# The unused tile ahead of the weight pool of a hybrid block's last stages: 96 bytes in place of 480

## The chip, the cores and the metric

The kernel runs on one core of a Trainium2 chip. The metric is the time of one execution on the device in microseconds; lower is better. Before the change three runs took 2,879.13 to 2,882.53 us, with a median of 2,881.99 us.

## What is computed

One layer of a diffusion backbone over 1,024 latent tokens and 256 context tokens with 1,024 channels. Per layer: a feed-forward part with half weight, a token mixer (grouped attention beside a gated linear recurrence, HGRN2, in both directions), and a second feed-forward part. Cut to what matters here:

```python
def swiglu(u, w_gate, w_up, w_down):
    return (jax.nn.silu(u @ w_gate) * (u @ w_up)) @ w_down
def merge(p, o_att, o_hg, w_att_out_l, w_hg_out_l, w_o_l):
    y = jax.nn.sigmoid(p[8]) * (o_att @ w_att_out_l) + jax.nn.sigmoid(p[9]) * (o_hg @ w_hg_out_l)
    return y @ w_o_l
...
x = x + ffn1(x, mx)
...
y_x, y_c = token_mixer(...)
x = x + post(y_x, norm_post[l, 1], mx[5])
...
x = x + ffn2(x, mx)
```

The hidden width of the feed-forward parts is 2,816, that is 22 slices of 128. The context tokens take part in the first feed-forward part and in the mixer; the merge and the second feed-forward part are computed for the latent tokens alone.

## The kernel before, in words

Activations lie transposed, channels on the 128 partitions and tokens along the free dimension, in chunks of 512, 512 and 256 (context) tokens. Every large product is made three times: operands are split into a high and a low part in the type float32r, and `term` (lines 98 to 102) issues high x high (line 100), high weight x low activation (line 101) and low weight x high activation (line 102). Each is one 128x128 stationary tile, loaded anew for each matmul, and a moving tile of 512 columns (256 for the context and for the last pieces). `load_w` (lines 86 to 93) fetches a weight of 128x1,024 floats with one DMA into the staging tile `st`, ScalarE casts the high part (line 91) and VectorE subtracts to get the low part (line 92); both are tiles `w` of 4,096 bytes a partition of the pool that is named by the caller.

The stages, in order: the first FFN (weights from the pool `w1`); the attention, with projections as fillers between its matmuls (`fb`, weights from `w1`); the HGRN stage, with the gate columns as fillers (`fb`, weights from the pool `hgw`); and the last stages, in which all weights come from the pool `ffn2w`: the merge (line 1046 on, moving tiles `h00` to `l11`, called `h` and `l` in the rows), the output projection `w_o` and the second FFN (moving tiles `uh`, `ul`, and `h` for the down projection). The merge begins when the last `fb` fillers are done. During the output projection the norms of the chunks that are done run beside it on VectorE, ScalarE and GpSimd (`Norms.chain`, lines 244 to 286; `cb`, `rc` and `acc` are their tiles), moved forward piece by piece by `nrm.pump()`; the second FFN of a chunk starts when its norm has written `uh` and `ul`. A Tile framework places the tiles, sets the waits and orders each engine's instructions; each engine works through its own queue.

**Where tiles lie.** Pools are stacks in each partition's memory: those without a side grow from the low addresses, those with `side="right"` from the top at byte 229,344 down. Lines 1039 to 1043 open the right stack of the last stages:

```python
    w2_ctx = ExitStack()
    edge = w2_ctx.enter_context(tc.tile_pool(name="edge", bufs=1, side="right"))
    edge.tile([P, 120], F32, name="edge")
    wp = w2_ctx.enter_context(tc.tile_pool(name="ffn2w", bufs=12, side="right", reuse_waits="tile"))
```

Nothing reads or writes the tile `edge`; it takes 480 bytes, from 228,864 to the top. Below it lie the twelve slots of `ffn2w`, from 179,712 to 228,864, each at a multiple of 512 bytes. The slots of `w1` lie from 83,328 to 124,288 and those of `hgw` from 83,328 to 99,712, each at a multiple of 512 plus 384. So do the moving tiles: `uh0` at 5,504, `uh1` at 21,888, `ul0` at 38,272, `ul1` at 54,656, the merge's `h` and `l` tiles from 103,808 on, the first FFN's `h` tiles from 136,576 on and the second's from 138,624 on: all leave 384 modulo 512. A stationary slice steps by 512 bytes within its slot, a moving slice by 2,048 bytes within its tile. The exceptions are the context's `uh2` and `ul2` (480 modulo 512, 256 columns). The highest tile of the left stack in the merge (`gt`) ends at 179,584. Before `ffn2w`, the memory of its slots belonged to tiles of the HGRN stage (`qt`, `q2`, `k1`, `qb`, `Sp`, `kt`, `s0`, `both`, `ss`, `sq`, `rr`); a new tile waits until the tiles that it covers are no longer read.

## Time and profile before

| what | value |
|---|---|
| median of three runs | 2,881.99 us |
| the profiled execution | 2,881.1 us |
| its span, first to last instruction | 2,879.3 us |
| mean granted TensorE clock | 0.982 |
| TensorE matmuls busy | 2,750.9 us, 96% |
| VectorE, ScalarE, GpSimd busy | 54%, 35%, 12% |

The profile is one execution. PE stands for TensorE's matmuls, PEld for its weight loads, DVE for VectorE, ACT for ScalarE, POOL for GpSimd, SP for the engine that issues DMAs. In rows of groups, `out<-in` are the program's tiles and x is the count. Matmuls are pipelined: the next one starts before the last one's row ends, so the distance between starts, not the length of a row, tells how fast they are taken.

### The profile page before, as it was taken

What the parts mean: (1) busy time and instruction counts of PE and PEld (TensorE: products, weight loads), DVE (VectorE), ACT (ScalarE), POOL (GpSimd) and SP (SyncE); (2) the same over time, 40 slices, a digit from 0 to 9 for tenths busy, and PEclk for the clock granted to TensorE, in tenths of its full rate; (3) what the DMA queues carried; (4) which work ended last, traced back from release to release, by engine and by line L of the source; (5) the groups of instructions that cost most, each with busy time, mean ns of one, the idle gap of its engine ahead of it and who ended that gap; (6) DMA issues with size and microseconds to landing.
All of it is one profiled execution on the core that took longest, in us unless ns stands there. A gap on an engine that the chain in (4) does not pass through costs nothing.

```text
span 2879.3 us, 37319 instructions
## 1 busy us (share of the span) xinstructions
PE 2750.9 (96%) x15032; PEld 2336.6 (81%) x15032; DVE 1543.3 (54%) x2893; ACT 1010.0 (35%) x1495; POOL 354.7 (12%) x276
## 2 busy tenths in 40 slices
PE   4799999999999989999999988899999999999998
PEld 3588888888888888889988877788778888888887
DVE  7756554444435885655654398645464333333336
ACT  3521111111112542667775565244354211111123
POOL 4700000000000332100000232212131000000002
PEclk9899999999999999999999999999999999999999
DMA  6553222332212332111111333164343211111123
GB/s 228 178 155 96 74 81 73 95 96 74 66 44 88 116 109 77 61 59 40 38 55 55 115 115 120 63 197 142 122 147 104 67 49 44 45 44 56 47 68 102
DMA packets 114702, 259.48 MB, mean 90 GB/s; under 512 B 12256, under 2 KB 51808, under 8 KB 114528
## 3 DMA queue, kind: packets, MB, share of 16 engines
q1 hardware_dynamic: 114528, 257.08, 28.3%
q8 instruction: 118, 1.93, 0.3%
q14 instruction: 56, 0.46, 0.0%
HBM read 216.67 MB, written 40.37 MB: 89 GB/s over the span
## 4 chain that ended last, share of the span: by engine, by line
PE 75%; DVE 9%; issue 8%; ACT 4%; POOL 2%; DMA 2%; SPq 0%; DVEq 0%; POOLq 0%; ACTq 0%
PE bank L101 13%; PE bank L102 13%; PE bank L100 13%; PE y L100 6%; PE y L101 6%; PE y L102 6%; PE fb L102 3%; PE fb L101 3%; PE fb L100 3%; PE S L749 2%; PE bank L765 1%; PE po L778 1%; PE po L779 1%; DVE acc L242 1%; DVE w L92 1%
## 5 line engine op out<-in xcount | busy, mean ns | idle before, releaser
L100 PE MATMUL bank<-uh,w 128*128 128x512 f32 (+1 forms) x1952 | 718.7, 369 | 17.2 <-ACT uh L460 14.7
L101 PE MATMUL bank<-ul,w 128*128 128x512 f32 (+1 forms) x1952 | 721.9, 370 | 6.8 <-POOL ul L461 6.8
L102 PE MATMUL bank<-uh,w 128*128 128x512 f32 (+1 forms) x1952 | 720.8, 369 | 2.1 <-DVE w L92 2.1
L91 ACT CAST w<-st 128x1024 fp32r<-128x1024 f32 x234 | 242.9, 1047 | 798.2 <-PE y L101 442.6
L100 PEld LDWEIGHTS bank<-uh,w 128*128 128x128 f32 x1952 | 370.7, 190 | 81.8 <-ACT uh L460 17.0
L101 PEld LDWEIGHTS bank<-ul,w 128*128 128x128 f32 x1952 | 372.0, 191 | 72.6 <-POOL ul L461 9.9
L102 PEld LDWEIGHTS bank<-uh,w 128*128 128x128 f32 x1952 | 372.5, 191 | 64.6 <-DVE w L92 2.7
L92 DVE TENSOR_TENSOR w<-st,w 128x1024 fp32r<-128x1024 f32 x212 | 267.9, 1271 | 260.2 <-ACT w L91 258.2
L355 DVE TENSOR_TENSOR y<-y,y 128x512 f32<-128x512 f32 (+1 forms) x416 | 255.1, 619 | 206.4 <-PE y L102 204.4
L100 PE MATMUL y<-h,w 128*128 128x512 f32 (+1 forms) x736 | 284.3, 389 | 8.0 <-ACT h L341 3.6
L101 PE MATMUL y<-h,w 128*128 128x512 f32 (+1 forms) x736 | 282.8, 384 | 0.3 <-DVE h L342 0.3
L102 PE MATMUL y<-h,w 128*128 128x512 f32 (+1 forms) x736 | 281.9, 384 | 0.6 <-DVE w L92 0.6
L340 DVE TENSOR_TENSOR sl<-bank,sl 128x512 f32<-128x512 f32 (+1 forms) x114 | 70.5, 620 | 380.3 <-PE bank L102 372.7
L268 POOL TENSOR_TENSOR y<-y,xt 128x512 f32<-128x512 f32 x48 | 64.2, 1355 | 1570.4 <-DVE y L267 885.5
L100 PE MATMUL fb<-uh,w 128*128 128x512 f32 (+1 forms) x576 | 222.4, 386 | 0.0
L102 PE MATMUL fb<-uh,w 128*128 128x512 f32 (+1 forms) x576 | 219.7, 381 | 0.0
L101 PE MATMUL fb<-ul,w 128*128 128x512 f32 (+1 forms) x576 | 219.7, 381 | 0.0
L100 PEld LDWEIGHTS y<-h,w 128*128 128x128 f32 x736 | 138.0, 188 | 42.0 <-ACT h L341 5.1
L102 PEld LDWEIGHTS y<-h,w 128*128 128x128 f32 x736 | 138.5, 189 | 29.6 <-DVE w L92 1.3
L101 PEld LDWEIGHTS y<-h,w 128*128 128x128 f32 x736 | 138.8, 189 | 26.7 <-DVE h L342 0.6
L341 ACT CAST h<-sl 128x512 fp32r<-128x512 f32 (+1 forms) x92 | 55.4, 602 | 283.9 <-DVE sl L340 283.7
L339 ACT ACTIVATE sl<-bank 128x512 f32<-128x512 f32 (+1 forms) x114 | 61.3, 539 | 191.2 <-PE bank L102 191.1
(225 smaller groups left out, 4315.9 us busy)
## 6 DMA issues: line engine op xcount, KB each, us to landing
st<-in_w_mod SPq DMA_DIRECT2D x77, 512.0 KB, 3.7
st<-in_w_gate SPq DMA_DIRECT2D x56, 512.0 KB, 3.7
st<-in_w_up SPq DMA_DIRECT2D x56, 512.0 KB, 3.7
st<-in_w_down SPq DMA_DIRECT2D x56, 512.0 KB, 3.6
st<-in_w_col SPq DMA_DIRECT2D x32, 512.0 KB, 3.7
gate_d<-ft SPq DMA_DIRECT2D x32, 256.0 KB, 2.3
gt<-gate_d SPq DMA_DIRECT2D x32, 256.0 KB, 2.7
st<-in_w_o SPq DMA_DIRECT2D x16, 512.0 KB, 3.7
```

The source lines that it names most:

```text
L91: act.copy(hi, st)
L92: eng.tensor_tensor(lo, st, f32(hi), op=ALU.subtract)
L100: pe.matmul(ps, lh, rh, start=first, stop=False)
L101: pe.matmul(ps, lh, rl, start=False, stop=False)
L102: pe.matmul(ps, ll, rh, start=False, stop=last)
L242: dve.tensor_tensor(a3, a3, sq, op=ALU.add)
L268: pool.tensor_tensor(yj, yj, xt, op=ALU.add)
L339: act.activation(sl, pg, AF.Silu)
L340: dve.tensor_tensor(sl, pu, sl, op=ALU.mult)
L341: act.copy(hh, sl)
L355: dve.tensor_tensor(yd, py, yd, op=ALU.add)
L749: pe.matmul(S[:, cs_], qT[:, (s * 2 + t) * P:(s * 2 + t + 1) * P], kT[g][:, cs_], start=(s == 0), stop=(s == 1))
```

## The change

The unused tile has 24 floats in place of 120, 96 bytes in place of 480. All slots of `ffn2w` move up by 384 bytes, to addresses that leave 384 modulo 512.

```diff
-    edge.tile([P, 120], F32, name="edge")
+    edge.tile([P, 24], F32, name="edge")
```

## Rows read from the trace of the kernel before

**Rows 1.** The page, part 1: busy time and share of the span.

```profile
PE 2750.9 (96%) x15032; PEld 2336.6 (81%) x15032; DVE 1543.3 (54%) x2893; ACT 1010.0 (35%) x1495; POOL 354.7 (12%) x276
```

**Rows 2.** By stretch: us; busy PE, PEld, DVE, ACT, POOL; granted clock, DMA share, GB/s.

```profile
1860.00:1985.00 125.00, 125.00 (x585) 103.61 (x584) 56.42 (x80) 50.09 (x71) 23.63 (x15) 1.00 0.52 167
...
2062.00:2177.00 115.00, 107.94 (x489) 88.15 (x487) 75.25 (x193) 67.16 (x112) 44.52 (x32) 0.94 0.44 138
2177.00:2790.00 613.00, 612.82 (x2637) 495.48 (x2636) 218.80 (x278) 109.01 (x142) 0.00 (x0) 1.00 0.18 55
```

**Rows 3.** Timeline of TensorE, first FFN: start us, length; the first and last of 83.

```profile
530.68 0.39 PE L100 MATMUL bank<-uh,w 128*128 128x512 f32 x1
...
549.27 0.39 PE L101 MATMUL bank<-ul,w 128*128 128x512 f32 x1
```

**Rows 4.** The same, last gate columns: the first and last of 54.

```profile
1905.00 0.39 PE L100 MATMUL fb<-uh,w 128*128 128x512 f32 x1
...
1917.02 0.40 PE L102 MATMUL fb<-uh,w 128*128 128x512 f32 x1
```

**Rows 5.** The same, merge: the first and last of 81.

```profile
1917.25 0.40 PE L100 MATMUL bank<-h,w 128*128 128x512 f32 x1
...
1935.85 0.39 PE L102 MATMUL bank<-h,w 128*128 128x512 f32 x1
```

**Rows 6.** The same, second FFN: the first and last of 174.

```profile
2299.79 0.39 PE L100 MATMUL y<-h,w 128*128 128x512 f32 x1
...
2340.00 0.39 PE L102 MATMUL bank<-uh,w 128*128 128x512 f32 x1
```

**Rows 7.** The same, first FFN, behind matmuls of 256 columns.

```profile
500.65 0.28 PE L102 MATMUL y<-hc,w 128*128 128x256 f32 x1
...
502.18 0.39 PE L102 MATMUL bank<-uh,w 128*128 128x512 f32 x1
...
502.64 0.40 PE L101 MATMUL bank<-ul,w 128*128 128x512 f32 x1
502.88 0.39 PE L102 MATMUL bank<-uh,w 128*128 128x512 f32 x1
...
503.57 0.39 PE L102 MATMUL bank<-uh,w 128*128 128x512 f32 x1
...
504.25 0.39 PE L102 MATMUL bank<-uh,w 128*128 128x512 f32 x1
...
505.61 0.39 PE L102 MATMUL bank<-uh,w 128*128 128x512 f32 x1
```

**Rows 8.** Groups of TensorE's matmuls by shape from 1,885 us on.

```profile
L100 PE MATMUL bank<-uh,w 128*128 128x512 f32 x800 | 317.7, 397 | 0.6 <-ACT sl L339 0.6
...
L100 PE MATMUL y<-h,w 128*128 128x512 f32 x336 | 133.0, 398 | 0.2 <-ACT h L341 0.2
...
L100 PE MATMUL bank<-h,w 128*128 128x512 f32 x128 | 50.5, 395 | 0.0
...
L102 PE MATMUL bank<-uh,w 128*128 128x256 f32 x64 | 18.0, 281 | 0.0
...
L101 PE MATMUL y<-h,w 128*128 128x256 f32 x32 | 9.1, 287 | 0.0
```

**Rows 9.** What TensorE waited for, 1,980 to 2,200 us.

```profile
PE cb L217 <- DVE rc L194: 3.8, 1, 3.8
PE bank L102 <- DVE w L92: 2.1, 1, 2.1
```

**Rows 10.** Timeline of TensorE behind the first of these waits.

```profile
2091.10 0.63 PE L102 MATMUL bank<-uh,w 128*128 128x512 f32 x1
...
2092.38 0.63 PE L102 MATMUL bank<-uh,w 128*128 128x512 f32 x1
```

**Rows 11.** Line 1021 on TensorE, and ScalarE's first cast of a merge weight.

```profile
L1021 PE MATMUL hb<-ident,sq x8: 270/272/273, 1883.7 to 1884.4; 128*128 128x128 f32 x8
...
1913.18 1.05 ACT L91 CAST w<-st 128x1024 fp32r<-128x1024 f32 x1 [1.18 <-DMA st<-in_w_mrg]
```

## The prediction

> **What bounds the kernel now.** I read the page's busy shares first, then the busy time by stretch, then the groups of the last stretch, and last the start times of single matmuls. TensorE is busy for 96% of the span [rows 1]. [...]

> A busy share of 100% doesn't say how fast the matmuls follow each other. They overlap (a row lasts 0.39 us, and the next one starts some 0.23 us after it), so what counts is the distance between two starts, the pitch. For matmuls of 512 columns I took it from four stretches that hold nothing else:
> - First FFN, from 530.68 to 549.27 us: 83 matmuls, 82 distances, 18.59 us, so 226.7 ns [rows 3].
> - Last gate columns (`fb`), from 1,905.00 to 1,917.02 us: 54 matmuls, 12.02 us over 53, so 226.8 ns [rows 4].
> - Merge, which begins right behind it, from 1,917.25 to 1,935.85 us: 81 matmuls, 18.60 us over 80, so 232.5 ns [rows 5].
> - Second FFN, from 2,299.79 to 2,340.00 us: 174 matmuls, 40.21 us over 173, so 232.4 ns [rows 6].

> The third and fourth lie on one side, the first and second on the other. Between the second and the third only a quarter of a microsecond passes. Both lie in one stretch at a granted clock of 1.00 [rows 2], and shape and type are the same; what changes is which tiles are read. The stationary tile comes from the pool `hgw` on the left in the second and from `ffn2w` on the right in the third. By the addresses given with the kernel, `hgw` and `w1` slots start at 384 modulo 512, like every moving tile of these four stretches, and `ffn2w` slots start at 0. All slices step by 512 or 2,048 bytes, so a slice has the remainder of its slot.

> A second trait goes with it. Where the remainders are equal, the pitch settles: behind a run of 256-column matmuls the starts 502.18 to 503.57 are 1.39 us for six distances, 231.7 ns each, and from 504.25 to 505.61 six distances take 1.36 us, 226.7 ns each [rows 7]. Where they are unequal, no such settling is left in a mean over 173.

> **The change, part by part.** The unused tile shrinks from 480 to 96 bytes. No instruction works on it, so nothing is added or removed on any engine or queue. The pool `ffn2w` is stacked below it and moves up by 384 bytes: its slots go from remainder 0 to 384, the remainder of the moving tiles `uh`, `ul`, `h` and of the merge's own `h` and `l` tiles. That is the whole change.

> *512-column matmuls of the last stages.* From 1,885 us on there are three lines each with 128 (merge), 800 (output projection, gate and up) and 336 (down) of them [rows 8]: 3 x 1,264 = 3,792. If they take the pitch of the equal stretches, each gains 232.45 - 226.75 = 5.7 ns. The sum is 3,792 x 5.7 ns = 21.6 us. The two ends for the pitch are 226.7 (settled) and 232.5 (nothing changes); I take the settled one, because the `fb` matmuls [rows 4] are nearest in time, with the same moving tiles `uh` and `ul` that the second FFN reads.

> *256-column matmuls.* There are 64 and 32 on each of three lines [rows 8], 288 in all. At the unequal remainders of now two of the groups have a mean length of 281 and 287 ns [rows 8]; a 256-column row at equal remainders lasts 0.28 us [rows 7]. No difference in length shows at this width, so I take 0, with 288 x 5.7 ns = 1.6 us more or less as an outer bound.

> *Settling.* After a break some ten matmuls run at about 231.7 instead of 226.7. The last stages have few breaks; eight of them would cost 8 x 10 x 5 ns = 0.4 us. I take 0.2.

> *The norm stretch, 2,062 to 2,177 us.* Here TensorE is busy for 107.94 of 115 us at a clock of 0.94 [rows 2]. It waits 3.8 us for VectorE's `rc` and 2.1 us for the split weights `w` [rows 9]. [...] The chain that it waits for runs on VectorE, ScalarE and GpSimd, which this change doesn't speed up. So what the matmuls of this stretch gain may turn into a longer wait. The stretch has 489 matmuls [rows 2], the norm's small ones among them; an estimate of 400 wide ones gives 400 x 5.7 ns = 2.3 us. Bounds: all kept, or all lost. I take half, 1.2 us lost, since there are full runs as well as waits in it. The chain begins only when the matmuls ahead are done, so what is gained before it is kept.

> *Memory that is taken over.* Shifted by 384 bytes, three weight slots lie over other remains of the HGRN stage: the second weight tile that the pool gives out now touches its `rr`, the third its `sq` and `ss`, the fourth its `both`. The last work that reads any of these is TensorE's transposes of `sq`, which start from 1,883.7 to 1,884.4 us [rows 11]. The first cast of a merge weight is at 1,913.18 us [rows 11], so 28 us cover that, and I cost it at nothing. Without that cover it would be a wait of ScalarE's cast behind the transposes, and the merge weights would be late.

> *Sum.* 21.6 - 0.2 - 1.2 = 20.2 us. The profiled execution took 2,881.1 us, 1.8 us more than its span of 2,879.3 us; 0.9 us less than the median of 2,881.99 us. From the median, 2,881.99 - 20.2 gives **2,861.8 us**.

> **Rivals.**
> *Nothing changes: the place counts, not the remainder.* All slow rows have weights from the right stack, above address 179,712, and all fast rows from the left, below 124,288. The trace has no 512-column row with weights on the right at an equal remainder, so it can't separate the two. What speaks against it: fast stretches fall into a regular pitch behind a break, which fits two streams of reads that run in step, and a place has no reason to make them do so. It would give 2,882 us. [...] I give this rival 0.10.

> *Slower: the streams lock at a bad phase.* With equal remainders the two streams could also fall into step where they collide most. The longest distance of the unsettled part is 0.24 us (502.64 to 502.88) [rows 7]. If all 3,792 kept that, they would cost (240 - 232.45) x 3,792 = 28.6 us, and the time would be 2,910.6 us. It counts as slower from a mean pitch of 234.0 ns on (5.8 us over 3,792). Against it: the same remainder settles at the good end in two stages with different slots [rows 3, 4]. I give it 0.03.

> *Part of the gain is lost in the norm stretch and by lower settling.* This lies in the range: with a pitch of 228.5 (a third of the matmuls at 231.7, the others at 226.75, makes 228.4) and all of the norm stretch lost, (232.45 - 228.5) x 3,392 = 13.4 us, so 2,868.6 us.

> **How the numbers follow.** A measurement of this kernel can tell about 0.2%, 5.8 us, from no change. Faster by more than that needs a mean pitch under 230.9 ns: 0.87. The first rival gives 0.10 for within 0.2%, the second 0.03 for slower. The range starts at 2,857: the full 21.6 us and 1.6 us from the narrow matmuls, and under 2 us as the three runs of before differ. It ends at 2,869, the partial case. It leaves out both rivals and little else.

> **What would show it.** Right: in the changed kernel, the merge behind the last `fb` matmul goes on at 226.7 ns; the stretch that lasted 613 us ends some 15 us earlier (2,637 instructions, nearly all 512 wide, by 5.7 ns); the stretch before 1,917 us is as it was; the waits [rows 9] are up to 2 us longer in sum. Wrong: the merge starts again at 232 ns (then the place decides), or its distances are regular but longer (a bad phase), or TensorE shows new idle time in the second FFN.

## The result and the profile after

The changed kernel takes 2,862.36 us (median of 4 runs, 2,860.32 to 2,865.86) where the kernel before takes 2,881.32 us (median of 4): a ratio of 0.9936, with a 95% interval of 0.9919 to 0.9954, so it is faster by 0.46% to 0.81%. The prediction said 2,861.8 us.

The profiled execution took 2,862.51 us, its span 2,860.7 us, 18.6 us less than before. It has the same 15,032 matmuls, and every engine has its instructions in the same order, but for a few small matmuls of the HGRN stage that start within a few hundredths of a microsecond of each other and stand in another order in the trace. The page, part 1, of the changed kernel:

```profile
span 2860.7 us, 37319 instructions
PE 2730.9 (95%) x15032; PEld 2332.9 (82%) x15032; DVE 1542.4 (54%) x2893; ACT 1009.6 (35%) x1495; POOL 352.8 (12%) x276
```

TensorE's busy time fell by 20.0 us [rows 1]; VectorE, ScalarE and GpSimd changed by 0.4 to 1.9 us. The timeline of TensorE in the changed kernel at the step from the last `fb` matmul to the merge (start us, length):

```profile
1917.20 0.39 PE L100 MATMUL fb<-uh,w 128*128 128x512 f32 x1
1917.43 0.39 PE L101 MATMUL fb<-ul,w 128*128 128x512 f32 x1
1917.65 0.39 PE L102 MATMUL fb<-uh,w 128*128 128x512 f32 x1
1917.88 0.39 PE L100 MATMUL bank<-h,w 128*128 128x512 f32 x1
1918.11 0.39 PE L101 MATMUL bank<-l,w 128*128 128x512 f32 x1
...
1919.92 0.39 PE L100 MATMUL bank<-h,w 128*128 128x512 f32 x1
```

The merge goes on as the fillers ran: nine distances from 1,917.88 to 1,919.92 us are 226.7 ns each, where 80 distances were 232.5 ns before [rows 5]. The second FFN, the first and the last of 178 matmuls in the same window as before:

```profile
2299.76 0.39 PE L100 MATMUL y<-h,w 128*128 128x512 f32 x1
...
2339.88 0.39 PE L101 MATMUL bank<-ul,w 128*128 128x512 f32 x1
```

40.12 us over 177 distances are 226.7 ns, where it was 232.4 ns [rows 6]. Behind 2,177 us, 96% of the distances between wide matmuls are now 226 or 227 ns; before, all but a few were spread over 228 to 241 ns.

Where the time came from is read best by setting the same matmul of two executions side by side. The first three rows of the table are the first matmuls of their stages, the last three are single matmuls: one behind the norm stretch, one near the end of the second FFN, and the last of all. For two later runs the table has only the difference to before. They are a repeat of the changed kernel (`after_again`) and the first experiment (`e1_left_shift`).

| matmul | before, us | after, us | after | repeat | left shift |
|---|---|---|---|---|---|
| merge | 1,917.25 | 1,917.88 | +0.63 | +0.36 | +1.30 |
| output projection | 2,006.48 | 2,007.10 | +0.62 | -1.84 | -0.89 |
| norm stretch (first `cb`) | 2,062.26 | 2,061.50 | -0.76 | -3.21 | -2.27 |
| second FFN, steady | 2,179.02 | 2,175.91 | -3.11 | -3.89 | -2.89 |
| second FFN, near its end | 2,790.07 | 2,772.50 | -17.57 | -18.32 | -17.24 |
| last | 2,871.41 | 2,852.70 | -18.71 | -19.43 | -18.34 |

At the merge the two executions of the changed kernel stand 0.6 and 0.4 us behind the one of before, the left shift 1.3 us. From the merge on, the gain is 19.3 us in the profiled execution, 19.8 in the repeat and 19.6 with the left shift; the prediction had 20.2. The merge itself gained nothing in the profiled execution: TensorE had a new wait there. Its waits from 1,915 to 2,062 us in the changed kernel (total us, times, longest), where the kernel before had none:

```profile
PE bank L100 <- DVE gt L1074: 1.3, 3, 0.6
```

### The profile page after: what moved, and what is told of

It is laid out like the page before. It is cut to its first block, busy times and chain, and to the rows that moved or that the text cites. A ratio compares the mean times of both kernels' runs of the same rounds, so it can differ in the third digit from the quotient of the medians.

```text
span 2860.7 us, 37319 instructions
## 1 busy us (share of the span) xinstructions
PE 2730.9 (95%) x15032; PEld 2332.9 (82%) x15032; DVE 1542.4 (54%) x2893; ACT 1009.6 (35%) x1495; POOL 352.8 (12%) x276
## 4 chain that ended last, share of the span: by engine, by line
PE 71%; DVE 10%; issue 8%; ACT 4%; DMA 4%; POOL 2%; SPq 0%; DVEq 0%; POOLq 0%; ACTq 0%
PE bank L101 12%; PE bank L102 12%; PE bank L100 12%; PE y L100 6%; PE y L101 6%; PE y L102 6%; PE fb L101 2%; PE fb L102 2%; PE fb L100 2%; PE S L749 2%; PE bank L765 1%; DMA gt<-gate_d 1%; PE po L778 1%; DVE w L92 1%; PE po L779 1%
```

## The experiments

All edits keep the computation. The bytes named are per partition; for the kernels marked "one run" there is a single time.

**The place or the remainder.** `e1_left_shift` leaves the weights of the last stages exactly where the kernel before has them (remainder 0) and moves the left stack, the moving tiles among it:

```diff
 # kernel before, edge stays [P, 120]
+    ctx.enter_context(tc.tile_pool(name="pad", bufs=1)).tile([P, 32], F32, name="pad")
     up = ctx.enter_context(tc.tile_pool(name="u", bufs=1))
```

> The unused tile keeps its 480 bytes, so the weights of the last stages lie where they lay before (remainder 0). A second unused tile of 128 bytes at the bottom of the left stack moves uh, ul, h, l and the slots of w1 and hgw up to remainder 0. Remainder theory: equal again everywhere, so the 512-column pitch of the last stages falls to 226.7 to 227.3 ns and the time to 2,862 us (2,858 to 2,868), without a weight of these stages having moved. Place theory (the weights' own address in the right stack sets the pitch): 232.4 ns and 2,881 us as before.

Measured: 2,860.68 us (median of 4), ratio 0.9927 with an interval of 0.9911 to 0.9944. The timeline of TensorE, the first and the last of 178 matmuls in the second FFN:

```profile
2299.78 0.39 PE L102 MATMUL y<-h,w 128*128 128x512 f32 x1
...
2339.90 0.39 PE L100 MATMUL bank<-uh,w 128*128 128x512 f32 x1
```

That is 40.12 us over 177, 226.7 ns. Not one weight of these stages moved, and the pitch is that of the changed kernel. The place theory falls.

**The other way round.** `e2_w1_off` starts from the changed kernel and makes gate and up of the first FFN unequal, while its down products, whose `h` and `w` move together, stay equal:

```diff
+    w1_ctx.enter_context(tc.tile_pool(name="pad", bufs=1)).tile([P, 32], F32, name="pad")
     w1 = w1_ctx.enter_context(tc.tile_pool(name="w1", bufs=10))
```

> Starts from the changed kernel; an unused tile of 128 bytes below the pool w1 moves w1 and the first FFN's h from remainder 384 to 0, uh and ul stay at 384. So in the first FFN the gate and up products are unequal (384 against 0) and the down products equal (0 and 0). Remainder theory: gate and up of the first FFN and the fillers that read w1, 2,784 matmuls of 512 columns, go from about 227 to 232.4 ns, the down products between them stay at 227 to 229, the last stages stay at 226.9; the time grows by up to 2,784 x 5.5 ns = 15 us, to 2,874 to 2,878 us. Place theory (left is fast, high right addresses are fast too, low right ones slow): nothing changes, 2,862 us.

Measured: 2,868.18 us (one run). The timeline of TensorE in the first FFN, the first and the last of 79 matmuls:

```profile
530.83 0.39 PE L102 MATMUL bank<-uh,w 128*128 128x512 f32 x1
...
548.96 0.39 PE L102 MATMUL bank<-uh,w 128*128 128x512 f32 x1
```

18.13 us over 78 distances, 232.4 ns, where it was 226.7 ns [rows 3]. The groups of matmuls by shape from 100 to 1,000 us show that only the unequal ones became longer (count | busy us, mean ns of one). The run:

```profile
L101 PE MATMUL bank<-ul,w 128*128 128x512 f32 x627 | 248.9, 397 | 0.0
...
L101 PE MATMUL y<-h,w 128*128 128x512 f32 x334 | 131.1, 392 | 0.0
```

The same two groups in the changed kernel:

```profile
L101 PE MATMUL bank<-ul,w 128*128 128x512 f32 x627 | 245.8, 392 | 0.0
...
L101 PE MATMUL y<-h,w 128*128 128x512 f32 x334 | 131.9, 395 | 0.0
```

So equal and unequal products stand side by side in one stage, and the pitch follows the operands. The price was mis-sized: 5.7 us at the end against the profiled execution of the changed kernel and 6.4 us against its repeat (`after_again`, below), where up to 15 were expected. In the first FFN the distances behind the 2,016 wide gate and up matmuls, waits included, grew by 8.9 us in sum against the first and by 9.7 us against the second, not by 11.5: those behind a 256-column run were unsettled anyway [rows 7], and the profiled execution of the changed kernel had a spell at a granted clock of 0.50 there (from 983.1 to 986.4 us; 0.91 in the mean from 980 to 1,000 us) that the other two had not. The context's 256-column matmuls became faster (runs of 48 at 118.2 to 118.4 ns, against 120.1), about 2 us together. Near 935 us the run was 5.8 us behind. What the fillers lost in the attention, 1.7 to 1.8 us, was mostly gone again by 1,731 us, in the HGRN stage.

**Which distances count.** Four sizes of the unused tile, one run each; the edit is the number in

```diff
-    edge.tile([P, 24], F32, name="edge")
+    edge.tile([P, 88], F32, name="edge")   # e3_off256; 32 in e4_off32, 8 in e8_off64, 56 in e9_off192
```

> The unused tile takes 352 bytes: the weights of the last stages leave 128 modulo 512, 256 from the moving tiles. If equality modulo 512 is what counts: a slow pitch, 230 to 236 ns, and 2,872 to 2,895 us. If equality modulo 256 is enough: 226.9 ns and 2,862 us. Place theory: between before and after, since the weights lie 128 bytes above those of before and 256 below those of after.

> The unused tile takes 128 bytes: the weights of the last stages leave 352 modulo 512, 32 less than the moving tiles. If the remainders must be equal: a slow pitch near 232 ns and about 2,880 us. If near is enough (a window of some tens of bytes): 226.9 to 228 ns and 2,862 to 2,866 us.

> The unused tile takes 32 bytes: the weights of the last stages leave 448 modulo 512, 64 more than the moving tiles. If only a distance of 0 modulo 256 settles: a slow pitch, 230 to 235 ns, and 2,875 to 2,888 us. If 64 is a period of its own: 226.9 ns and 2,862 us.

> The unused tile takes 224 bytes: the weights of the last stages leave 256 modulo 512, 128 less than the moving tiles, where the kernel before has 128 more. If the distance counts modulo 256, the two are the same: 232.4 to 232.6 ns, spread over 228 to 241, and 2,880 us. If it counts modulo 512, another pitch may show.

The timelines of TensorE from 2,300 to 2,340 us, the first and the last of 178 matmuls in `e3_off256`:

```profile
2299.74 0.39 PE L100 MATMUL bank<-uh,w 128*128 128x512 f32 x1
...
2339.91 0.39 PE L100 MATMUL bank<-uh,w 128*128 128x512 f32 x1
```

of 173 in `e4_off32`:

```profile
2299.76 0.39 PE L102 MATMUL y<-h,w 128*128 128x512 f32 x1
...
2339.89 0.39 PE L100 MATMUL bank<-uh,w 128*128 128x512 f32 x1
```

of 174 in `e8_off64`:

```profile
2299.62 0.40 PE L100 MATMUL y<-h,w 128*128 128x512 f32 x1
...
2339.99 0.40 PE L100 MATMUL bank<-uh,w 128*128 128x512 f32 x1
```

and of 173 in `e9_off192`:

```profile
2299.83 0.40 PE L102 MATMUL bank<-uh,w 128*128 128x512 f32 x1
...
2339.82 0.39 PE L100 MATMUL bank<-uh,w 128*128 128x512 f32 x1
```

| stationary minus moving address, modulo 512 | kernel | pitch, ns | time, us |
|---|---|---|---|
| 0 | after, left shift | 226.7 | 2,862.4, 2,860.7 |
| 256 | `e3_off256` | 227.0 | 2,865.5 |
| 64 | `e8_off64` | 233.4 | 2,878.3 |
| 128 | before | 232.4 | 2,881.3 |
| 384 | `e9_off192` | 232.5 | 2,884.1 |
| 480 | `e4_off32` | 233.3 | 2,882.3 |

A distance of 256 is as good as 0 within 0.3 ns (227.0 and 226.7), and 128 and 384 are alike (232.4 and 232.5); so these six fit a distance that counts modulo 256, not 512. Other distances were not tried. Near is not enough: 32 bytes off is slow (233.3 ns). The 3 us by which `e3_off256` is longer than the changed kernel don't come from the last stages: at the 5,001st matmul, near 1,021 us and ahead of any address that differs, that execution was 2.9 us behind the one of before. From 980 to 1,000 us its granted clock was 0.83, and 1.00 before.

**The wait in the merge, and the context's matmuls.** The changed kernel once more, two kernels that move the context's operands `uh2` and `ul2`, and one with more room for `gt`:

```diff
 # e5_uc: 24 floats; e6_uc32: 32 floats
+    uc_ctx.enter_context(tc.tile_pool(name="pad", bufs=1, side="right")).tile([P, 24], F32, name="pad")
     ucp = uc_ctx.enter_context(tc.tile_pool(name="uc", bufs=1, side="right"))
 # e7_gt6 alone
-    wp = w2_ctx.enter_context(tc.tile_pool(name="ffn2w", bufs=12, side="right", reuse_waits="tile"))
+    wp = w2_ctx.enter_context(tc.tile_pool(name="ffn2w", bufs=11, side="right", reuse_waits="tile"))
-                    gt = mp.tile([P, 512], F32, name="gt", bufs=5)
+                    gt = mp.tile([P, 512], F32, name="gt", bufs=6)
```

> The changed kernel once more, to stand beside the next two on one chip: 2,862 us (2,859 to 2,866). In the merge the wait for a free PSUM bank (released by VectorE's product with gt, which waits for the DMA of gt) comes and goes with the DMA's timing, so it may show between 0 and 2 us.

> The changed kernel with an unused tile of 96 bytes above the context's uh2 and ul2, which moves them from 480 to 384 modulo 512, the remainder of w1. If 256-column matmuls also settle at equal remainders, the matmuls of 256 columns of the first FFN and the fillers stay at 120 ns and the unsettled ones behind them become fewer, worth up to 2 us: 2,860 us. If the width is too short for it: no change, 2,862 us.

> The same with 128 bytes, so uh2 and ul2 leave 352 and the weights 32 more, the distance at which the run with w1 moved had 118.2 to 118.5 ns at 256 columns where the changed kernel has 120.0 to 120.9. If that distance is what did it: 1.5 to 2 ns on about 1,250 matmuls, 2 us less, 2,860 us, with 118.4 ns in the first FFN. If it was something else there: 120 ns and 2,862 us.

> The changed kernel with six gt tiles in place of five; ffn2w gives up one of twelve slots for the room. If the merge lost its gain because VectorE's release of the PSUM banks waits for gt's DMA, which waits for a free gt tile: the waits of TensorE in the merge (three of 0.5 to 0.7 us in the changed kernel) go, the merge ends up to 2 us earlier, and the time is 2,860 to 2,862 us. If the waits come from the order of the DMA queue: they stay. Eleven weight slots may bring a wait for a slot instead, seen at line 91 or 92.

`after_again` took 2,861.13 us (median of 5; ratio 0.9938, 0.9925 to 0.9950). TensorE has no wait in its merge, and the merge gained 2.20 us, 384 matmuls by 5.7 ns. So the wait of the profiled execution comes and goes between executions of one program. That it hangs on the DMA's timing is argued from the chain from 1,940 to 1,990 us (49% of it is `gt`'s load), not shown.

`e5_uc` took 2,859.34 us (0.9932, 0.9919 to 0.9944), `e6_uc32` 2,861.29 us (0.9932, 0.9919 to 0.9946); the intervals overlap that of the repeat almost wholly, so neither can be told from the changed kernel. The pitch at 32 did what was expected. In `e6_uc32` a run of 48 context matmuls, first and last:

```profile
521.06 0.28 PE L100 MATMUL bank<-uh,w 128*128 128x256 f32 x1
...
526.62 0.28 PE L102 MATMUL bank<-uh,w 128*128 128x256 f32 x1
```

in `e5_uc`, where the remainders are equal:

```profile
520.58 0.28 PE L100 MATMUL bank<-uh,w 128*128 128x256 f32 x1
...
526.22 0.28 PE L102 MATMUL bank<-uh,w 128*128 128x256 f32 x1
```

and in the changed kernel:

```profile
522.12 0.28 PE L100 MATMUL bank<-uh,w 128*128 128x256 f32 x1
...
527.77 0.28 PE L102 MATMUL bank<-uh,w 128*128 128x256 f32 x1
```

5.56, 5.64 and 5.65 us over 47 distances: 118.3, 120.0 and 120.2 ns. In `e5_uc` nearly all single distances in the first FFN are 120 ns, while in the changed kernel they are spread over 115 to 125: the narrow matmuls do settle at equal remainders, but that gains next to nothing. From 174 to 845 us, in the first FFN, `e5_uc` gained 0.6 us and `e6_uc32` 1.3 us on the repeat; near 935 us they had lost 1.4 and 1.5 us again. In both this lies behind a wait of TensorE of 2.4 us for `h`, which the repeat has too: the granted clock was lower behind it (0.66 from 926 to 936 us, 0.83 in the repeat), and the norm's eight one-column matmuls that follow started 0.21 us apart where they start 0.11 us apart in the repeat.

`e7_gt6` took 2,867.31 us (one run). The merge has no wait, but neither has the repeat with five tiles, so this tells nothing of the sixth. With eleven weight slots TensorE waits more behind 2,062 us, 14.8 us in sum against 10.7 in the repeat; two of its waits there, of which the repeat has the first of 0.5 us and the second not at all at this line:

```profile
PE y L100 <- ACT h L341: 3.5, 1, 3.5
...
PE y L102 <- DVE w L92: 1.0, 1, 1.0
```

## Why the prediction was right

*What bounds it.* The last stages did follow TensorE's pitch alone from 2,179 to 2,790 us: 611.05 us became 596.59 us, 14.46 us less for 2,629 matmuls, 5.50 ns each. In the changed kernel TensorE is busy for 613.00 of the 613 us from 2,177 to 2,790 us, and the granted clock is 1.00, as before [rows 2].

*The pitch.* 5.7 ns was the right size: 232.4 to 226.7 ns in the same window. From 2,179 to 2,790 us it is 5.50 ns: without the few distances over 0.3 us, gate and up have a mean of 226.7 ns and the down products one of 227.3, so the term of 0.2 us for what is not settled was too small by about 0.5 us.

*The cause.* The first rival, the place, is refuted by `e1_left_shift` and `e2_w1_off` together: a stage is made fast without moving its weights, and another is made slow by moving its weights alone. The second rival, a bad phase, did not occur at any equal remainder that was run. The runs show 5.7 ns a matmul (232.4 ns before, 226.7 ns after and with the left shift) that the two operands' addresses alone set; what the time is spent on no run shows. Why a distance of 0 or 256 gives 226.7 to 227.0 ns and the others 232.4 to 233.4 was not measured; that two streams of reads run in step was my guess, and no run shows them.

*The merge.* The prediction priced the merge by TensorE's pitch alone. In the profiled execution it had a second bound close behind: 2.2 us of gain turned into three waits for the release of a PSUM bank (1.3 us idle; counted by starts, the three waits and the matmul behind each took 2.0 us more). In the repeat they were absent.

*The norm stretch.* I took 1.2 of 2.3 us as lost. In the repeat and with the left shift this stretch gained 0.68 and 0.62 us. There was less to gain than I priced: of the 397 wide matmuls here only 347 were followed by another wide one within 0.3 us, and these distances shrank by 1.6 us in sum in the repeat, not by 2.3. And 0.7 us became longer waits: TensorE's waits from 1,980 to 2,200 us sum to 7.3 us before and to 8.0 us in the repeat. The waits that the prediction named are still there, in the profiled execution of the changed kernel:

```profile
PE cb L217 <- DVE rc L194: 4.0, 1, 4.0
PE bank L102 <- DVE w L92: 1.8, 1, 1.8
```

They were 3.8 and 2.1 us before [rows 9]. Yet in this execution the stretch gained 2.35 us, 1.67 more than in the repeat. The waits hardly explain that: theirs differ by 0.3 us. Sixty matmuls, around the wait for `rc` and behind it, took 1.4 us less, 16.79 us for 18.19. Their stretches, with the columns of [rows 2], first in the profiled execution and then in the repeat:

```profile
2079.21:2096.00 16.79, 12.79 (x62) 10.49 (x60) 13.77 (x42) 7.97 (x12) 4.12 (x3) 0.90 0.83 273
2076.76:2094.95 18.19, 14.18 (x62) 11.77 (x60) 13.77 (x42) 7.97 (x12) 4.11 (x3) 0.81 0.78 252
```

The granted clock was 0.90 there and not 0.81. In the profiled execution it was 0.50 from 2,089.0 to 2,092.3 us, with distances of 0.43 us between wide matmuls (2,089.33 to 2,091.89 is 2.56 us for six), and 1.00 from 2,092.4 us to the end of that stretch; the kernel before had 0.50 from 2,088.6 to 2,095.3 us, with the same distances [rows 10]. Why the spells differ in length is not shown. So that execution lost 2.2 us in the merge, and the sixty matmuls at a higher granted clock gave back 1.4; that its gain from the merge on came within 1 us of the predicted 20.2 is in part luck. In the repeat the merge kept its gain and the norm stretch kept 0.7 us, where the prediction had 1.1.

*Nothing else moved.* The 256-column matmuls of the last stages stayed at about 120 ns, and the casts of the merge's first weights waited for their DMAs alone (6.8 us in sum from 1,905 to 1,935 us, the same as before), not for the HGRN tiles that the slots now cover.

## What to carry to other kernels

## What was not expected

In these runs the distance fits a count modulo 256, while the change was stated modulo 512. The slow distances are not alike: 32 and 64 bytes off (233.3 and 233.4 ns) are slower than 128 off (232.4 and 232.5 ns). At 256 columns the order is another: with the stationary tile 32 bytes above the moving one the pitch is 118.3 ns, with the changed kernel's 416 it is 120.1 to 120.2 ns, and at equal remainders (`e5_uc`) it is 119.8 to 120.0 ns. So an equal remainder is the best distance that was tried, with 256, for the wide matmuls, and worse by 1.5 to 1.7 ns than 32 for the narrow ones; 32 above was not tried for the wide ones. Executions differ by 1 to 3 us where their granted clocks differ: `e3_off256` and the kernel before by 2.9 us at about 1,021 us, ahead of what the edit touches (0.83 from 980 to 1,000 us, 1.00 before), and two executions of one kernel by 1.4 us over the 60 matmuls above (0.90 and 0.81); to judge a change of this size, compare stretches at the same granted clock.
